# Latent attention with two sets of buffers and outputs through DRAM, and the triangular inverses' round trip on GpSimd's queue

## The chip, the cores and the metric

One core of one Trainium2 chip. The time is the device time of one execution in microseconds (us). An execution of the kernel before was timed three times; a further one was recorded by the profiler, and all rows below are from that one.

## What is computed

Two blocks of a small transformer on 256 tokens of width 2048, in float32. The first block (two layers of convolution and window attention) is not touched. The second block normalises, projects, runs two mixers on halves of the projection, joins their outputs in one out-projection and ends with a gated feed-forward part:

```python
proj = rms_norm(x, g) @ w_in
y_rwkv = rwkv7_mixer(...)     # 16 heads of 64: a recurrence over the tokens, group norm, gate
y_mla = mla_mixer(...)        # latent attention, 8 heads of 128, causal softmax
x = x + concatenate([y_rwkv, y_mla], -1) @ w_out      # 2048 -> 2048
...
# inside mla_mixer: q and k, v are projections of two latents c_q, c_kv of width 512
sc = (q_nope @ k_nope.T + q_pe @ k_pe.T) * scale
out = softmax(where(causal, sc, -1e30)) @ v           # for each head, in blocks of 128 queries
```

## The kernel before

Every large product is made in three passes: a weight tile comes from DRAM on SyncE's queue (`wraw`), ScalarE casts it to its high part `whi` (L285), VectorE subtracts to get the low part `wlo` (L286), and TensorE multiplies high by high, high by low and low by high. `lin` does so with 256 moving columns (L327 to L329), `wide` with the high and low half of the moving operand side by side (L347) and one pass for the low weights (L350). A moving operand is kept as such a pair of halves, a `Split`, in slots of 8 KB per partition; there are 8 slots (`slot`, tag x8), which the stages hand on to each other.

The function `mixers` makes the projection and both mixers. The recurrence goes over four groups G of four heads: `rwkv_lin` projects, `rwkv_prepare` makes the matrices of a group, among them, by `tri_inverse`, the inverses of small triangular matrices, and `rwkv_chunks` runs the four chunks of 64 tokens one after the other, each a chain of small matmuls (`pch`, L1106 to L1122) with copies on ScalarE between. `tri_inverse` writes the matrices to a DRAM buffer `xd` and reads them back in another layout as `L` (L1044, L1049, L1050), does 31 steps on VectorE (L1058, L1059; the starting `T` is loaded at L1053), writes the result to `td` (L1061), reads it back as `Tc` (L1063) and transposes it (L1064). These are 14 DMAs per group, 56 in all, issued by ScalarE: xd<-Lc is one of 1024 rows of 128 bytes, L<-xd are four of 32 rows and four of 512, td<-T four of 256 rows and Tc<-td one of 1024.

A group's output is gated by the product `pgt` (L1163, L1165), stored to the DRAM buffer `ydr` (L1166) and loaded back in `load_y` (L833), where `split_pair` makes the two halves: a cast on ScalarE (L271) and a subtraction on VectorE (L272). The four head pairs of the latent attention are made by `mla_pair`: projections, scores `msc` (L1306, L1307), the exponential and the scaling on ScalarE (L1313, L1318), transposes `mtr` (L1322), the products with the values `mo` (L1327 to L1329), and a copy of each head's output out of PSUM (L1330). All pairs work in the same two slots, `mla_s`, so one pair's buffers are let go before the next takes them. A pair's output `yp` is split straight from SBUF into its place in `Ym`.

The out-projection is `rows`: for each of eight column blocks j it multiplies first Ym (k = 0 to 7), then the first six tiles of Yr (the recurrence's output), and last, behind `load_y(3)`, tiles 6 and 7 by `lin`. It adds to the residual `h2`, two slots of 1 MB, loaded from `hdr` (L827) and scaled on VectorE (L829).

Instructions are put in order by a scheduler that runs when the program is built: it plays the program through on a model of the engines and writes one fixed order for each engine. The order in time on a queue is then that order; an instruction that waits holds back all that stand behind it on its engine. Parts of the recurrence have a higher priority in it (`high_priority`).

## Time and profile before

| | |
|---|---|
| median of three executions | 2218.68 us (2218.06 to 2219.01) |
| the profiled execution | 2222.46 us |
| its span, first to last instruction | 2220.7 us |
| mean granted clock of TensorE, share of full speed | 0.991 |
| TensorE busy | 2182.3 us, 98% |
| VectorE busy | 1698.3 us, 76% |
| ScalarE busy | 1186.7 us, 53% |
| GpSimd busy | 106.7 us, 5% |
| DMA traffic | 412.83 MB, 186 GB/s |

Engines are PE (TensorE), PEld (its weight loads), DVE (VectorE), ACT (ScalarE), POOL (GpSimd) and SP (SyncE); ACTq is ScalarE's queue as it issues DMAs. A line number is one of the kernel file. In timelines the square brackets give the idle time ahead of an instruction on its engine, and behind the arrow what ended it. Issuing a DMA isn't counted as busy on ScalarE.

### The profile page before, as it was taken

What the parts mean: (1) busy time and instruction counts of PE and PEld (TensorE: products, weight loads), DVE (VectorE), ACT (ScalarE), POOL (GpSimd) and SP (SyncE); (2) the same over time, 40 slices, a digit from 0 to 9 for tenths busy, and PEclk for the clock granted to TensorE, in tenths of its full rate; (3) what the DMA queues carried; (4) which work ended last, traced back from release to release, by engine and by line L of the source; (5) the groups of instructions that cost most, each with busy time, mean ns of one, the idle gap of its engine ahead of it and who ended that gap; (6) DMA issues with size and microseconds to landing.
All of it is one profiled execution on the core that took longest, in us unless ns stands there. A gap on an engine that the chain in (4) does not pass through costs nothing.

```text
span 2220.7 us, 37351 instructions
## 1 busy us (share of the span) xinstructions
PE 2182.3 (98%) x14263; PEld 1972.0 (89%) x14263; DVE 1698.3 (76%) x3140; ACT 1186.7 (53%) x1825; POOL 106.7 (5%) x253
## 2 busy tenths in 40 slices
PE   8999999999999999999999999999999999999998
PEld 8999988889999888899999887888888888888887
DVE  6999999778989988787777885777765576556765
ACT  6456746554456555656665655355443444444443
POOL 3100000000000000002100000010000000000000
PEclk9999999999999999999999998999999999999999
DMA  7875556665565466777665433576656666566654
GB/s 232 245 207 165 175 166 223 191 210 179 183 184 167 153 198 212 218 219 222 192 169 140 122 106 102 167 255 203 190 185 195 193 189 190 190 192 189 189 191 141
DMA packets 374514, 412.83 MB, mean 186 GB/s; under 512 B 40456, under 2 KB 327429, under 8 KB 373952
## 3 DMA queue, kind: packets, MB, share of 16 engines
q1 hardware_dynamic: 336464, 366.06, 53.6%
q0 software_dynamic: 10960, 31.79, 4.5%
q10 hardware_dynamic: 26912, 12.60, 2.6%
q8 instruction: 112, 1.84, 0.3%
q14 instruction: 66, 0.54, 0.1%
HBM read 390.47 MB, written 19.92 MB: 185 GB/s over the span
## 4 chain that ended last, share of the span: by engine, by line
PE 93%; DVE 3%; DMA 2%; ACT 1%; issue 1%; ACTq 0%; SPq 0%; DVEq 0%
PE wide L347 30%; PE wide L350 15%; PE lin L327 7%; PE lin L328 7%; PE lin L329 7%; PE lin L1393 3%; PE lin L1394 3%; PE lin L1392 3%; PE dn L1393 2%; PE dn L1394 2%; PE dn L1392 2%; PE po L701 1%; PE lin L1225 1%; PE lin L1223 1%; PE lin L1224 1%; DVE wlo L286 1%
## 5 line engine op out<-in xcount | busy, mean ns | idle before, releaser
L285 ACT CAST whi<-wraw 128x1024 fp32r<-128x1024 f32 (+1 forms) x708 | 724.8, 1026 | 837.7 <-PE wide L347 329.5
L286 DVE TENSOR_TENSOR wlo<-wraw,whi 128x1024 fp32r<-128x1024 f32 (+1 forms) x708 | 843.8, 1193 | 357.2 <-ACT whi L285 341.3
L347 PE MATMUL wide<-xs,whi 128*128 128x512 f32 x2916 | 745.7, 394 | 3.9 <-ACT whi L285 2.0
L347 PEld LDWEIGHTS wide<-xs,whi 128*128 128x128 f32 x2916 | 521.3, 189 | 95.0 <-ACT whi L285 2.5
L350 PEld LDWEIGHTS wide<-xs,wlo 128*128 128x128 f32 x2916 | 402.7, 190 | 33.0 <-DVE wlo L286 1.9
L350 PE MATMUL wide<-xs,wlo 128*128 128x256 f32 x2916 | 416.4, 283 | 0.4 <-DVE wlo L286 0.2
L329 PE MATMUL lin<-xs,wlo 128*128 128x256 f32 x1420 | 404.9, 285 | 2.2 <-DVE wlo L286 2.2
L327 PE MATMUL lin<-xs,whi 128*128 128x256 f32 x1420 | 405.5, 286 | 0.9 <-ACT whi L285 0.9
L328 PE MATMUL lin<-xs,whi 128*128 128x256 f32 x1420 | 404.7, 285 | 0.0
L329 PEld LDWEIGHTS lin<-xs,wlo 128*128 128x128 f32 x1420 | 273.5, 193 | 3.3 <-DVE wlo L286 2.6
L327 PEld LDWEIGHTS lin<-xs,whi 128*128 128x128 f32 x1420 | 273.4, 193 | 3.1 <-ACT whi L285 1.3
L328 PEld LDWEIGHTS lin<-xs,whi 128*128 128x128 f32 x1420 | 273.5, 193 | 1.1 <-issue 0.7
L583 DVE SCALAR_TENSOR_TENSOR cy<-apad,vc_cw,cy 128x256 f32<-128x256 f32 x480 | 229.7, 481 | 7.5
L1393 PE MATMUL lin<-wlo,xs 128*128 128x512 f32 (+1 forms) x304 | 117.7, 387 | 0.5 <-DVE wlo L286 0.5
L1394 PE MATMUL lin<-whi,xs 128*128 128x512 f32 (+1 forms) x304 | 117.0, 385 | 0.0
L1392 PE MATMUL lin<-whi,xs 128*128 128x512 f32 (+1 forms) x304 | 114.1, 386 | 0.2 <-ACT whi L285 0.2
L1393 PEld LDWEIGHTS lin<-wlo,xs 128*128 128x128 f32 x304 | 57.2, 188 | 11.9 <-DVE wlo L286 1.2
L1392 PEld LDWEIGHTS lin<-whi,xs 128*128 128x128 f32 x304 | 57.2, 188 | 11.6 <-ACT whi L285 0.6
L1392 PE MATMUL dn<-whi,xs 128*128 128x512 f32 (+1 forms) x176 | 67.0, 381 | 0.0
L1393 PE MATMUL dn<-wlo,xs 128*128 128x512 f32 (+1 forms) x176 | 67.0, 381 | 0.0
L1394 PE MATMUL dn<-whi,xs 128*128 128x512 f32 (+1 forms) x176 | 67.0, 381 | 0.0
L1394 PEld LDWEIGHTS lin<-whi,xs 128*128 128x128 f32 x304 | 57.2, 188 | 11.0
(540 smaller groups left out, 2374.4 us busy)
## 6 DMA issues: line engine op xcount, KB each, us to landing
wraw<-in_w_in_dram SPq DMA_DIRECT2D x244, 512.0 KB, 4.1
wraw<-in_w_out_dram SPq DMA_DIRECT2D x89, 512.0 KB, 4.2
wraw<-in_ffn_w_gate_dram SPq DMA_DIRECT2D x88, 512.0 KB, 4.4
wraw<-in_ffn_w_up_dram SPq DMA_DIRECT2D x88, 512.0 KB, 3.7
wraw<-in_ffn_w_down_dram SPq DMA_DIRECT2D x87, 512.0 KB, 3.9
wraw<-in_w_pg_dram SPq DMA_DIRECT2D x64, 512.0 KB, 4.3
bt<-btab POOLq DMA_DIRECT2D x32, 192.0 KB, 3.2
btab<-bF ACTq DMA_DIRECT2D x4, 1024.0 KB, 7.9
```

The lines of the kernel that those rows point to most:

```text
L285: nc.scalar.copy(hi[:], src)
L286: self.lo = nc.vector.tensor_tensor(lo[:], src, hi[:].bitcast(F32), ALU.subtract)
L327: nc.tensor.matmul(ps[:, t, :], lhsT=h, rhs=xh_, start=((t, k) == first), stop=False)
L328: nc.tensor.matmul(ps[:, t, :], lhsT=h, rhs=xl_, start=False, stop=False)
L329: nc.tensor.matmul(ps[:, t, :], lhsT=l, rhs=xh_, start=False, stop=((t, k) == last))
L347: nc.tensor.matmul(ps[t][:], lhsT=hi[:, i, ts], rhs=S.both(k).rearrange("p u c -> p (u c)"), start=(k == kts[0]), stop=False)
L350: nc.tensor.matmul(ps[t][:, :SEQ], lhsT=lo[:, i, ts], rhs=S.hi(k), start=False, stop=(k == kts[-1]))
L583: prev, tail = tail, nc.vector.scalar_tensor_tensor(y, ap[:, t, k : k + SEQ], cw[:, k : k + 1], y, ALU.mult, ALU.add)
L701: nc.tensor.matmul(po[:, qb, g, :], lhsT=pT[:, kb, qb * 128 : qb * 128 + 128], rhs=vd[:, kb, j, :], start=(kb == 0), stop=(kb == 1))
L1392: nc.tensor.matmul(ps, lhsT=zh, rhs=hi, start=(k == 0), stop=False)
L1393: nc.tensor.matmul(ps, lhsT=zh, rhs=lo, start=False, stop=False)
L1394: nc.tensor.matmul(ps, lhsT=zl, rhs=hi, start=False, stop=(k == nt - 1))
```

## The change

It does three things. The 14 DMAs of `tri_inverse` are issued by GpSimd in place of ScalarE. The latent attention gets two sets of its two slots, taken in turn by the pairs, and a pair's output is no longer split from SBUF: GpSimd stores it to a new DRAM buffer `mdr`, and `load_y` loads it back and splits it, for all four pairs ahead of the first three groups of Yr. The slots are taken in another order: Ym, h2, Yr behind the four slots of the attention, where it was mla, Ym, Yr, h2. An unused function is taken out, by which the lines behind it move up by 8 and, behind the new lines, by 5.

```diff
--- before.py
+++ after.py
...
@@ -812,28 +804,31 @@
         with self.tc.high_priority(offset=self.RP):
             self.rwkv_chunks(3, last)
         cq, ck = self.cqk
-        self.mla_s = self.slot(F32, "mla"), self.slot(F32, "mla")
-        Ym = self.new_split(2)
+        self.mla_s = [(self.slot(F32, "mla"), self.slot(F32, "mla")) for _ in range(2)]
+        self.mdr = self.dr.tile([128, 8, SEQ], F32, name="mdr")
         rf = self.wk.tile([128, SEQ], F32, tag="r", bufs=1, name="rf")
         self.bcast(self.rfc[:], None, out=rf)
         for hp in range(4):
-            self.mla_pair(hp, cq, ck, Ym)
+            self.mla_pair(hp, cq, ck)
 
         wo = A["w_out_2"][0]
+        Ym = self.new_split(2)
+        h2 = [self.slot(F32, "h2") for _ in range(2)]
         Yr = self.new_split(2)
-        h2 = [self.slot(F32, "h2") for _ in range(2)]
 
         for u in range(2):
             nc.gpsimd.dma_start(h2[u][:], self.hdr[:, 8 * u : 8 * u + 8, :])
             for k in range(8):
                 nc.vector.scalar_tensor_tensor(h2[u][:, k, :], h2[u][:, k, :], self.fg[:, 8 * u + k : 8 * u + k + 1], rf[:],
                                                ALU.mult, ALU.mult)
-        def load_y(G):
+        def load_y(G, dst, src):
             yt = self.sqt()
-            nc.gpsimd.dma_start(yt[:], self.ydr[:, 2 * G : 2 * G + 2, :])
-            self.split_pair(Yr, 2 * G, yt[:])
+            nc.gpsimd.dma_start(yt[:], src[:, 2 * G : 2 * G + 2, :])
+            self.split_pair(dst, 2 * G, yt[:])
+        for G in range(4):
+            load_y(G, Ym, self.mdr)
         for G in range(3):
-            load_y(G)
+            load_y(G, Yr, self.ydr)
         def rows(k0, k1, j, Y, row0=0):
             hh = self.at(h2, 2 * j, 2)
             if k1 - k0 < 4:
@@ -847,7 +842,7 @@
         late = 7
         for j in range(late):
             rows(0, 6, j, Yr)
-        load_y(3)
+        load_y(3, Yr, self.ydr)
         vf = self.vf
         self.x2 = self.dr.tile([128, KD, SEQ], F32, name="x2")
         self.XF = self.new_split()
@@ -1041,13 +1036,13 @@
         small = lambda s, tag="tri": self.wk.tile([128, 8, 32], F32, tag=tag, name=self.nm(s))
         Lc = small("Lc")
         nc.vector.tensor_tensor(Lc[:], AB[:, :, 0:32], AB[:, :, 32:64], ALU.add)
-        nc.scalar.dma_start(xd[:].rearrange("(c q) j i -> (q j) c i", q=4), Lc[:])
+        nc.gpsimd.dma_start(xd[:].rearrange("(c q) j i -> (q j) c i", q=4), Lc[:])
         L = self.wk.tile([128, 768], F32, tag="L", bufs=1, name=self.nm("L"))
         L0, L1 = L[:, 0:512].rearrange("p (j i) -> p j i", i=32), L[:, 512:768].rearrange("p (j i) -> p j i", i=16)
         for q in range(4):
             qs = slice(32 * q, 32 * q + 32)
-            nc.scalar.dma_start(L0[qs], xd[:, 0:16, :])
-            nc.scalar.dma_start(L1[qs], xd[:, 16:32, 16:32])
+            nc.gpsimd.dma_start(L0[qs], xd[:, 0:16, :])
+            nc.gpsimd.dma_start(L1[qs], xd[:, 16:32, 16:32])
         T, tmp = small("T"), small("Tt")
         o, n = CB["tinit"]
         nc.gpsimd.dma_start(T[:], self.A["c_blk"][:, o : o + n].rearrange("p (c i) -> p c i", c=8))
@@ -1058,9 +1053,9 @@
             nc.vector.tensor_tensor(tmp[:, 0:n, 0:m], lj, tj, ALU.mult)
             nc.vector.tensor_tensor(T[:, 0:n, j + 1 : 32], T[:, 0:n, j + 1 : 32], tmp[:, 0:n, 0:m], ALU.add)
         for q in range(4):
-            nc.scalar.dma_start(td[:, :, q, :], T[32 * q : 32 * q + 32, :, :])
+            nc.gpsimd.dma_start(td[:, :, q, :], T[32 * q : 32 * q + 32, :, :])
         Tc, Tt = small("Tc", "trc"), small("Ttr", "trc")
-        nc.scalar.dma_start(Tc[:], td[:].rearrange("(c h) e q i -> (h e q) c i", h=4))
+        nc.gpsimd.dma_start(Tc[:], td[:].rearrange("(c h) e q i -> (h e q) c i", h=4))
         nc.vector.transpose(Tt[:], Tc[:])
         return Tc, Tt
 
@@ -1246,12 +1241,12 @@
             hs = slice(64 * h, 64 * h + 64)
             nc.vector.tensor_tensor(kz[hs, h, :], tk[hs, 0, :], tk[hs, 1, :], ALU.add)
 
-    def mla_pair(self, hp, cq, ck, Y):
+    def mla_pair(self, hp, cq, ck):
 
         nc, A = self.nc, self.A
         wq, wkv = A["mla_w_uq_2"][0], A["mla_w_ukv_2"][0]
         cos, sin, kz, rc = self.cos, self.sin, self.kz, self.rkvc
-        s1, s2 = self.mla_s
+        s1, s2 = self.mla_s[hp % 2]
         qn, qp, kn, vn = (s1[:, 2 * u : 2 * u + 2, :] for u in range(4))
         yp, sh, pTs = s2[:, 0:2, :], [s2[:, 2:4, :], s2[:, 4:6, :]], s2[:, 6:8, :]
         scale = 192.0 ** -0.5
@@ -1328,7 +1323,7 @@
             nc.tensor.matmul(po[:, 128:256], lhsT=vn[:, 0, hs], rhs=pT[:, 0, 128:256], start=True, stop=False)
             nc.tensor.matmul(po[:, 128:256], lhsT=vn[:, 1, hs], rhs=pT[:, 1, 128:256], start=False, stop=True)
             nc.scalar.copy(yp[:, h, :], po[:])
-        self.split_pair(Y, 2 * hp, yp)
+        nc.gpsimd.dma_start(self.mdr[:, 2 * hp : 2 * hp + 2, :], yp)
 
 
     def ffn(self):
```

How the order of the instructions moves, at three places. First TensorE where the first pairs' outputs meet the out-projection. Before (`xs_14851` is the slot of Ym that holds k = 0 to 3, `mla_14850` and `mla_14849` the two slots of the pairs, `pch` the chunk chain of the last group):

```order
L347 MATMUL wide_15622<-xs_14851,whi_15628 128x512 x4
L350 MATMUL wide_15622<-xs_14851,wlo_15629 128x256 x3
L1322 MATMUL mtr_15393<-cblk,mla_14850 128x128 x2
L350 MATMUL wide_15622<-xs_14851,wlo_15629 128x256
L1106 MATMUL pch_14702<-rv,l_10987 128x64 x4
L1327 MATMUL mo_15374<-mla_14850,mla_14849 128x128
L1328 MATMUL mo_15374<-mla_14850,mla_14849 128x128
L1329 MATMUL mo_15374<-mla_14850,mla_14849 128x128
L347 MATMUL wide_15672<-xs_14851,whi_15678 128x512 x4
```

After (`xs_15585` is that slot of Ym; `mla_14849`, `mla_14850` are the first set and `mla_14851`, `mla_14852` the second; the first three rows end the attention of pair 1, and `msc_15378` are scores of pair 2; the two wide rows in the middle have k = 0 and 1, the last three k = 2 and 3):

```order
L1322 MATMUL mo_15217<-mla_14852,mla_14851 128x128
L1323 MATMUL mo_15217<-mla_14852,mla_14851 128x128
L1324 MATMUL mo_15217<-mla_14852,mla_14851 128x128
L1301 MATMUL msc_15378<-mla_14849 128x128
L1302 MATMUL msc_15378<-rope,mla_14849 128x128
L347 MATMUL wide_15637<-xs_15585,whi_15643 128x512 x2
L347 MATMUL wide_15687<-xs_15585,whi_15693 128x512 x2
L1301 MATMUL msc_15378<-mla_14849 128x256
L1302 MATMUL msc_15378<-rope,mla_14849 128x256
L347 MATMUL wide_15637<-xs_15585,whi_15643 128x512 x2
L350 MATMUL wide_15637<-xs_15585,wlo_15644 128x256 x4
L347 MATMUL wide_15687<-xs_15585,whi_15693 128x512 x2
```

The out-projection's matmuls on pair 1's output stand two scores and four matmuls behind that output's last matmul. Before, the first of them stood beside the last pair's attention and the chunk chain.

Second the queue of GpSimd at the same stretch. Before, the stores and loads of the recurrence with the residual's loads (h_2282, h_2283) behind the third store:

```order
L1166 DMA ydr<-sq_13236 128x512
L833 DMA sq_15614<-ydr 128x512
L1158 DMA ga_14839<-in_rwkv_g_2_dram 128x256
L1159 DMA ga_14839<-in_rwkv_g_2_dram 64x256
L1166 DMA ydr<-sq_14620 128x512
L827 DMA h_2282_15590<-hdr 128x2048
L827 DMA h_2283_15591<-hdr 128x2048
L833 DMA sq_15618<-ydr 128x512
L1166 DMA ydr<-sq_14810 128x512
L833 DMA sq_16316<-ydr 128x512
```

After:

```order
L1161 DMA ydr<-sq_13236 128x512
L820 DMA h_2282_15587<-hdr 128x2048
L1326 DMA mdr<-mla_14850 128x512
L820 DMA h_2283_15588<-hdr 128x2048
L826 DMA sq_15609<-mdr 128x512
L1326 DMA mdr<-mla_14852 128x512
L826 DMA sq_15613<-mdr 128x512
L1056 DMA td_14333<-T_14346 256x1x32 x4
L1153 DMA ga_14839<-in_rwkv_g_2_dram 128x256
L1154 DMA ga_14839<-in_rwkv_g_2_dram 64x256
L1161 DMA ydr<-sq_14620 128x512
L1326 DMA mdr<-mla_14850 128x512
```

The residual's two loads stand ahead of the load of the first pair's output and of the next pair's store; the third group's store of ydr now follows behind td.

Third TensorE where the last group's output meets the out-projection. Before, the product pgt of group 3 stood between wide matmuls on Ym:

```order
L347 MATMUL wide_15972<-xs_14852,whi_15998 128x512 x2
L1163 MATMUL pgt_14842<-hg,ga_14839 128x256 x4
L347 MATMUL wide_15972<-xs_14852,whi_15998 128x512 x2
L347 MATMUL wide_15973<-xs_14852,whi_15998 128x512 x4
```

After (`xs_15590` is the slot of Yr with k = 4 to 7):

```order
L350 MATMUL wide_16289<-xs_15590,wlo_16316 128x256 x2
L350 MATMUL wide_16290<-xs_15590,wlo_16316 128x256 x2
L1158 MATMUL pgt_14842<-hg,ga_14839 128x256 x4
L327 MATMUL lin_16340<-xs_15590,whi_16343 128x256
L327 MATMUL lin_16366<-xs_15590,whi_16369 128x256
L327 MATMUL lin_16394<-xs_15590,whi_16397 128x256
L328 MATMUL lin_16340<-xs_15590,whi_16343 128x256
```

The first LIN on the output of group 3 (tiles 6 and 7) follows directly behind that group's pgt; before, 60 rows stood between them.

## Rows read from the trace of the kernel before

**Rows 1.** The windows view: five engines in stretches of 100 us. Columns: the stretch; its length, then for TensorE (PE), its weight loads (PEld), VectorE (DVE), ScalarE (ACT) and GpSimd (POOL) the busy us and, in brackets, the instructions; then the granted clock of TensorE, the share of the DMA engines and GB/s.

```profile
1000.00:1100.00 100.00, 99.66 (x814) 97.70 (x813) 74.92 (x140) 63.04 (x95) 17.76 (x45) 1.00 0.74 213
1100.00:1200.00 100.00, 98.07 (x858) 94.27 (x857) 81.06 (x253) 61.59 (x105) 5.34 (x13) 0.98 0.58 154
1200.00:1300.00 100.00, 94.37 (x825) 84.03 (x824) 77.70 (x242) 59.93 (x126) 8.35 (x17) 0.95 0.42 112
1300.00:1400.00 100.00, 93.27 (x670) 81.45 (x669) 67.55 (x190) 52.04 (x122) 3.22 (x6) 0.90 0.40 124
```

**Rows 2.** The timeline of TensorE, those rows between 1100 and 1400 us with idle time ahead of them that the prediction names. Columns: start and duration in us, engine, line, operation, what it writes and reads, count; in square brackets the idle us ahead and what ended it.

```profile
1150.04 0.66 PE L1019 MATMUL ptn<-cblk,k__1748_12045 128*128 128x128 f32 x4 [1.41 <-DVE l L1034]
...
1210.11 0.39 PE L329 MATMUL lin<-xs,wlo 128*128 128x256 f32 x1 [1.64 <-DVE wlo L286]
...
1266.48 0.33 PE L1322 MATMUL mtr<-cblk,mla 128*128 128x128 f32 x1 [1.27 <-ACT mla L1318]
...
1280.39 0.93 PE L1114 MATMUL pch<-ch,tx 64*64 64x64 f32 x8 [1.31 <-ACT Y L1111]
...
1326.63 0.49 PE L1306 MATMUL msc<-mla 128*128 128x128 f32 x2 [0.92 <-DVE mla L1277]
1328.37 0.55 PE L1223 MATMUL lin<-ck,whi 128*128 128x256 f32 x1 [1.25 <-ACT mla L1297]
...
1337.19 1.11 PE L1163 MATMUL pgt<-hg,ga 128*128 128x256 f32 x3 [0.55 <-ACT sq L1155]
...
1363.59 0.84 PE L1322 MATMUL mtr<-cblk,mla 128*128 128x128 f32 x3 [1.86 <-ACT mla L1318]
1365.57 0.49 PE L1327 MATMUL mo<-mla,mla 128*128 128x128 f32 x2 [1.14 <-ACT mla L1324]
...
1367.62 1.97 PE L1106 MATMUL pch<-rv,l 128*128 128x64 f32 x8 [0.75 <-DVE rv L1129]
```

**Rows 3.** The timeline again, of VectorE (the first two rows) and of ScalarE. ACTq is the part of ScalarE's queue that issues DMAs.

```profile
1208.72 0.19 DVE L1058 TENSOR_TENSOR Tt<-L,T 128x31 f32<-128x31 f32 x1 [4.95 <-DMA L<-xd]
1208.83 1.22 DVE L286 TENSOR_TENSOR wlo<-wraw,whi 128x1024 fp32r<-128x1024 f32 x1
...
1259.86 2.56 ACTq L1061 DMA_DIRECT2D td<-T  x4
1262.74 0.40 ACT L1313 ACTIVATE mla<-mla,mst 128x128 f32<-128x128 f32 x1
...
1324.95 1.25 ACTq L1061 DMA_DIRECT2D td<-T  x2
1326.23 1.29 ACTq L1061 DMA_DIRECT2D td<-T  x2
1327.57 0.37 ACT L1330 COPY mla<-mo 128x256 f32<-128x256 f32 x1 [1.34 <-issue]
1327.83 0.48 ACT L1297 ACTIVATE mla<-lin,rkvc 128x256 f32<-128x256 f32 x1
```

**Rows 4.** The view of one buffer, of td and then of xd (the DRAM buffers of the inverse's round trip): line, queue, count, and the duration of one issue in ns (least, median, most).

```profile
L1061 ACTq DMA_DIRECT2D td<-T x16: 571/628/638, 1130.5 to 1326.9; - x16
L1063 ACTq DMA_DIRECT2D Tc<-td x4: 378/385/392, 1137.0 to 1332.1; - x4
...
L1049 ACTq DMA_DIRECT2D L<-xd x16: 308/497/1618, 1076.1 to 1285.7; - x16
L1050 ACTq DMA_DIRECT2D L<-xd x16: 322/445/832, 1076.8 to 1286.2; - x16
L1044 ACTq DMA_DIRECT2D xd<-Lc x4: 377/422/492, 1073.5 to 1279.2; - x4
```

**Rows 5.** The page's first part, GpSimd's row (busy us, share, instructions); the timeline of GpSimd, an issue of 128 rows; and the view of the buffer pr, whose load has 256 rows.

```profile
PE 2182.3 (98%) x14263; PEld 1972.0 (89%) x14263; DVE 1698.3 (76%) x3140; ACT 1186.7 (53%) x1825; POOL 106.7 (5%) x253
...
1070.37 0.54 POOL L1053 DMA_DIRECT2D T<-in_c_blk_dram  x1
...
L718 POOL DMA_DIRECT2D pr<-in_p_dram x2: 740/740/740, 17.5 to 254.9; - x2
```

**Rows 6.** The timeline around the last of the four round trips of a chunk group's output through DRAM, 256 KB, with a split behind it: TensorE, GpSimd (store and load), ScalarE, VectorE, and TensorE where the split is first read.

```profile
1414.68 2.00 PE L347 MATMUL wide<-xs,whi 128*128 128x512 f32 x8
...
1417.94 2.47 PE L1163 MATMUL pgt<-hg,ga 128*128 128x256 f32 x8
...
1421.69 0.55 POOL L1166 DMA_DIRECT2D ydr<-sq  x1 [62.83 <-DVE sq L1165]
1424.77 0.54 POOL L833 DMA_DIRECT2D sq<-ydr  x1 [2.53 <-DMA ydr<-sq]
...
1428.98 0.62 ACT L271 CAST xs<-sq 128x512 fp32r<-128x512 f32 x1 [1.22 <-DMA sq<-ydr]
...
1429.63 0.69 DVE L272 TENSOR_TENSOR xs<-sq,xs 128x512 fp32r<-128x512 f32 x1
...
1452.18 0.28 PE L327 MATMUL lin<-xs,whi 128*128 128x256 f32 x1
```

**Rows 7.** The view of the buffer hdr (the residual in DRAM): its loads, 1 MB each, and the landing times of its stores and loads; and the view of line 829, which scales what was loaded.

```profile
L827 POOL DMA_DIRECT2D h<-hdr x2: 534/536/537, 1342.5 to 1343.1; - x2
...
DMA to landing us min/median/max: 2.4/5.5/9.0
...
L829 DVE SCALAR_TENSOR_TENSOR h<-h,vc_a,rf x16: 475/478/480, 1359.4 to 1366.8; 128x256 f32<-128x256 f32 x16
```

**Rows 8.** The view of line 903, the longest copy that VectorE makes between buffers in this stage.

```profile
L903 DVE COPY rx<-rkt x4: 418/420/427, 1056.7 to 1261.5; 128x512 f32<-128x512 f32 x4
```

More of the change, by code (lines that the diff above doesn't have):

```diff
@@ L476, in bias_src @@
         return flat[127 : 127 + 128 * NREL].rearrange("(q c) -> q c", c=NREL)[:, :384]
-    def silu_pair(self, ps, r2, tag, bufs=2):
-        nc = self.nc
-        z = self.wk.tile([128, 2, SEQ], F32, tag=tag, bufs=bufs, name=self.nm("z"))
-        nc.vector.tensor_tensor(z[:], ps[:], r2, ALU.mult)
-        nc.scalar.activation(z[:], z[:], AF.Silu)
-        return z
     def gated(self, pv, pg, r2, other):
```

## The prediction

> **What bounds the kernel now.** I read the windows of 100 us first, then TensorE's idle times in the slow ones, and last the queues and the round trips that stand behind them. Outside the mixers of the second block TensorE has no gaps worth the name and its granted clock is at full speed, as in the window that begins at 1000 us (99.66% busy, clock 1.00) [rows 1]. In 1100 to 1400 it is idle for 1.93 + 5.63 + 6.73 = 14.3 us and the granted clock averages 0.98, 0.95 and 0.90 [rows 1]. At those clocks busy time of 98.07, 94.37 and 93.27 us does what full clock would do in 96.1, 89.7 and 83.9: some 16 us are lost to the clock. So at most 14.3 + 16 = 30 us can come back from this stage, and everything else is TensorE work that the change leaves as it is: the weight passes are the same.
>
> The idle times are short and each has its own releaser [rows 2]. Six of them, 7.0 us together, fall at 1150.04, 1210.11, 1266.48, 1326.63, 1328.37 and 1337.19; one of 1.31 us at 1280.39 stands inside the chunk chain; three, 1.86 + 1.14 + 0.75 = 3.75 us, stand at 1363 to 1368, in the attention of the last pair. Part of the six goes back to the triangular inverse's round trip on ACT's queue. At 1259.86 ACT's sequencer issues four DMAs for 2.56 us, and the exponential behind them starts at 1262.74; the transposes at 1266.48 wait for that chain. At 1324.95 and 1326.23 it issues 1.25 + 1.29 us, and the scaling at L1297 that releases TensorE at 1328.37 starts at 1327.83 [rows 3]. DVE, being in order, waits 4.95 us at 1208.72 for L<-xd [rows 3], and the wlo at 1210.11 that TensorE waits for stands right behind it.
>
> **The change, part by part.**
>
> *56 issues leave ACT.* 16 x 0.628 + 4 x 0.385 + 16 x 0.497 + 16 x 0.445 + 4 x 0.422 = 28.3 us of ACT's queue [rows 4]. ACT's own work has slack on the whole, so what this returns is the part of the six idle times that such an issue or its wait ended: between 0 and 7.0 us. I take 6, near the upper end, because at three of them the rows show the issue or the wait directly ahead. The wait for L<-xd doesn't vanish, but in the new order DVE has other work in that place. The clock returns some of its 16 us: the windows show the lower clock in the stretches that have these idle times. Of 1200:1300 and 1300:1400 (4.7 + 9.3 us) those of the chunk chain and of the last pair's attention keep theirs; I take 6 of 0 to 16.
>
> *The same 56 on GpSimd.* GpSimd is busy 5% of the span [rows 5], so the time is there; what counts is its order. A 128-row issue takes 0.54 us there, one of 256 rows 0.74 [rows 5]. L<-xd, td<-T and Tc<-td move tiny rows, up to 1024 of 128 bytes, and no row shows such an issue on this queue: at the lower end they stay at 0.74 us, by the slope between the two (0.20 us for 128 rows) a 1024-row one takes 1.9, in proportion to the rows 3.0. I take the slope, since two of the fourteen DMAs in a group reach that size; the round trip of the inverse is then some 2 to 3 us longer per group. For three of four groups it has tens of us of other work around it and costs nothing; if that cover is gone it costs its full length. For the last it is part of the next term.
>
> *Attention, its outputs by way of DRAM (the first two places of the order).* Before, a pair's output is split from SBUF into hi and lo straight behind the copy out of PSUM. Now it is copied (0.37 us [rows 3]), stored by GpSimd, loaded, cast on ACT and subtracted on DVE. The chunk groups' outputs make a round trip of this form and size; of the last one the store ydr<-sq is issued at 1421.69, the load at 1424.77, the cast starts at 1428.98 and the subtraction ends at 1430.32 [rows 6]: 8.6 us, 9.0 with the copy. The new order puts WIDE with k = 2, 3 (the second pair) only four WIDE and four score matmuls behind that pair's last output: 4 x 0.25 [rows 6] + 2 x 0.49 [rows 2] = 2.0 us of work to hide 9.0. That alone is 7.0 us of idle TensorE. The queue ahead of it makes it worse. On GpSimd the load of the residual's second half (1 MB) stands ahead of the loads of both pairs, and it waits for the last chunk group but one to let go of its buffer; the two loads of this kind landed after up to 9.0 us [rows 7]. On DVE its eight scalings, 8 x 0.478 us [rows 7], stand ahead of the low half of the first pair and of pair 2's score maxima. 9.0 + 3.8 = 12.8 us against some 6 us of TensorE work is 7 us more, but it runs at the same time as the round trip: I take 9 for the two (7.0 to 14). The last pair's round trip has 6 us of matmuls behind it, so 3 more. And the attention of pairs 2 and 3 now runs with next to no chunk steps between: the last pair alone cost 3.75 us that way before [rows 2], I take 8 for two (4 to 8). That is 20 us, less the 3.75 that are there already: **+16** (+3 to +21).
>
> *The last chunk group's output (third place).* The pgt matmuls of group 3 used to end 34 us ahead of the first LIN on Yr's k = 6, 7 (1417.94 to 1452.18 [rows 6]). The order now puts that LIN directly behind pgt. Its path is DVE's product, store, load, cast, subtraction: issue 1421.69 minus pgt's end 1420.41, plus 8.6 [rows 6], some 9.9 us, of which the first cast's products can start a little earlier: **+9** (7 to 11).
>
> *The clock after the new idle times.* Behind the idle times of now the granted clock falls to 0.90 over the window 1300:1400 [rows 1], 9.3 us for 6.7 us of idle time. The new ones are longer but in two places only. I take +3 (0 to 9).
>
> *The rest at nothing*: the two more buffers are slots of the same pool that lie free or are let go by then, and the order of the weight stream is unchanged; if a buffer came free later, the wait would be at the residual's loads, which is counted.
>
> Sum: -6 - 6 + 16 + 9 + 3 = **+16**. The profiled execution took 2222.46 us (span 2220.7), 3.8 above the median of the runs, 2218.68; the difference goes on the median: **2235**. About 0.2% (4.4 us) can be told from no change, so the bounds are 2214.2 and 2223.1.
>
> By the Trainium skill ("SBUF — State Buffer", section "SBUF: two separate sides") a DMA issued from GpSimd has its descriptors written by GpSimd's cores, which are locked out while DVE runs a copy or cast in its two-port mode, and one issued from ACT or SP is not. The trace so far does not bear it out: issues on this queue take 0.53 to 0.54 us [rows 5, 7] with DVE 68 to 75% busy [rows 1]. The longest DVE copy between buffers takes 0.42 us [rows 8]; by the rule 56 issues that each met one would take an estimated 24 us more, of which only what lies ahead of TensorE counts.
>
> **The rivals.**
>
> A, faster. The gains come in full (7 + 16 = 23 us) and the attention's term is nearly free, because with buffers of their own the pairs' scores and exponentials run ahead of TensorE and the order's closeness is not closeness in time. For it: the four WIDE with k = 0, 1 also wait, and so pair 1's trip can lie under that wait. Against: that wait is idle time itself. With +4 for that term and +9 at LIN the time is 2218.7 - 23 + 13 = 2209. It decides as long as that term is below 9.6 us (23 - 9 - 4.4).
>
> B, slower still. The moved issues are slow, by the number of rows or because DVE keeps them waiting. In proportion to rows (0.74 us for 256) a group's fourteen take 17.0 us (3.0 + 3.0 + 4 x 0.74 + 4 x 1.48 + 4 x 0.54), 9.9 more than the 7.1 on ACT; with GpSimd in order the stores of Y, the residual's loads and the pairs' trips are late by it. If 5 us of that show in three groups, 2235 + 15 = 2250. Against: the issues of now are flat.
>
> C, about the same. The attention's term at +8, since the residual's load is early enough, gains of 8 + 10, LIN +9: 2218.7 - 18 + 17 + 2 = 2220.
>
> That the change would not do what it says is excluded by the order: 56 issues fewer on ACT's queue, 64 more on GpSimd's.
>
> **How the numbers follow.** The forecast has 0.60, A 0.12, B 0.16, C 0.12. Faster by over 0.2% is A: 0.12. Same is most of C and a tail of the forecast: 0.13. Slower: 0.75. The forecast's own bounds are -23 to +44 with every term at an end, which no one case gives; with terms halfway to their ends it is 2222 to 2250. The range takes in C and most of B and leaves out A and B's tail: 2216 to 2256.
>
> **What would show it.** Right: two idle times of 7 us or more, at WIDE on the second pair's output and at the first LIN behind pgt, both released by the low or high half of xs; 1100 to 1300 at 99% busy and clock near 1.00; ACT's queue without L1044 to L1063; GpSimd waiting for DMAs. Wrong: the LIN of k = 6, 7 starting within 3 us of pgt; the idle times of 1150 to 1337 unchanged (then ACT's queue was not their cause); GpSimd's issues of L<-xd above 1.9 us (B); more idle time at the chunk chain than before.

## The result and the profile after

The changed kernel takes 2236.32 us (median of four runs, 2233.81 to 2239.04); before takes 2218.37 beside it. The ratio is 1.0081, with 95% confidence 1.0067 to 1.0094: 15 to 21 us slower. The profiled execution took 2233.96 us with a span of 2232.2, so the two traces differ by 11.5 us, less than the medians do: the trace of before is of an execution 4.1 above the median beside the change, that of after 2.4 below.

The windows of after, columns as in [rows 1]:

```profile
1100.00:1200.00 100.00, 100.00 (x892) 96.82 (x891) 83.91 (x252) 66.46 (x112) 18.08 (x34) 1.00 0.57 159
1200.00:1300.00 100.00, 95.00 (x839) 84.22 (x838) 78.96 (x231) 57.71 (x120) 20.83 (x37) 0.98 0.41 121
1300.00:1400.00 100.00, 87.16 (x589) 74.08 (x590) 64.26 (x195) 48.46 (x115) 11.91 (x21) 0.88 0.44 140
1400.00:1500.00 100.00, 88.45 (x531) 76.44 (x530) 72.06 (x138) 45.36 (x70) 11.21 (x23) 0.95 0.53 169
```

and the one of before that wasn't shown:

```profile
1400.00:1500.00 100.00, 97.04 (x571) 83.74 (x569) 77.08 (x141) 49.05 (x73) 12.33 (x25) 1.00 0.66 215
```

Against [rows 1] the time from 1100 to 1200 has no idle time left (1.93 before), 1200 to 1300 has 5.00 (5.63), 1300 to 1400 has 12.84 (6.73) and 1400 to 1500 has 11.55 (2.96). That is 12.1 us more idle time. Busy time times what the clock lacks is 0 + 1.9 + 10.5 + 4.4 = 16.8 us, against 2.0 + 4.7 + 9.3 + 0 = 16.0: in these two executions the clock as a whole gave nothing back.

By stage, idle time and clock together, the two traces differ by -7.3 us from 1100 to 1300, +7.2 from 1300 to 1400 and +13.0 from 1400 to 1500.

TensorE's waits in those windows, as in [rows 2] (with pgt of the last group, which doesn't wait, ahead of the last):

```profile
1240.51 0.38 PE L1218 MATMUL lin<-cq,whi 128*128 128x256 f32 x1 [2.18 <-ACT whi L285]
...
1278.94 0.39 PE L1220 MATMUL lin<-ck,wlo 128*128 128x256 f32 x1 [1.09 <-DVE wlo L286]
...
1332.37 2.07 PE L347 MATMUL wide<-xs,whi 128*128 128x512 f32 x4 [5.71 <-DVE xs L272]
...
1337.97 1.22 PE L347 MATMUL wide<-xs,whi 128*128 128x512 f32 x2 [1.82 <-DVE xs L272]
...
1354.31 1.17 PE L1317 MATMUL mtr<-cblk,mla 128*128 128x128 f32 x4 [2.05 <-ACT mla L1313]
...
1372.41 2.08 PE L347 MATMUL wide<-xs,whi 128*128 128x512 f32 x4 [2.01 <-DVE xs L272]
...
1451.14 2.47 PE L1158 MATMUL pgt<-hg,ga 128*128 128x256 f32 x8
1461.85 1.01 PE L327 MATMUL lin<-xs,whi 128*128 128x256 f32 x3 [8.23 <-ACT xs L271]
```

The six idle times of [rows 2] at 1150 to 1337 are gone, 7.0 us; others stand in 1200 to 1300, 5.0 us together, the longest at 1240 and 1279. The new ones are at WIDE on the first and second pair's output (5.71 + 1.82), at the transposes of the last pair (2.05), at WIDE on the last pair's output (2.01) and, directly behind pgt, at LIN (8.23). What runs on VectorE ahead of the first of them, with ScalarE's cast of the first pair's output to its high half as the last row:

```profile
1320.71 0.48 DVE L822 SCALAR_TENSOR_TENSOR h<-h,vc_a,rf 128x256 f32<-128x256 f32 x1 [1.05 <-DMA h<-hdr]
...
1321.18 2.84 DVE L822 SCALAR_TENSOR_TENSOR h<-h,vc_a,rf 128x256 f32<-128x256 f32 x7
...
1327.27 3.25 DVE L822 SCALAR_TENSOR_TENSOR h<-h,vc_a,rf 128x256 f32<-128x256 f32 x8
1330.55 0.42 DVE L1303 CUSTOM_DVE_ANT_0 mla<-msc,cblk 128x256 f32<-128x256 f32 x1
...
1331.64 0.68 DVE L272 TENSOR_TENSOR xs<-sq,xs 128x512 fp32r<-128x512 f32 x1
...
1327.26 0.62 ACT L271 CAST xs<-sq 128x512 fp32r<-128x512 f32 x1 [2.20 <-DMA sq<-mdr]
```

The residual's scalings (h<-h) take 0.48 + 2.84 + 3.25 us here, and the last eight stand in one piece ahead of the second score maximum and of the low half that WIDE waits for (1331.64). The cast that this low half needs had ended at 1327.88, 3.8 us sooner. GpSimd over the same time:

```profile
1312.54 0.55 POOL L820 DMA_DIRECT2D h<-hdr  x1 [16.60 <-PE lin L1220]
1313.08 0.54 POOL L1326 DMA_DIRECT2D mdr<-mla  x1
1319.60 0.53 POOL L820 DMA_DIRECT2D h<-hdr  x1 [5.98 <-PE pch L1101]
1321.77 0.54 POOL L826 DMA_DIRECT2D sq<-mdr  x1 [1.63 <-DMA mdr<-mla]
```

The second load of the residual waits 5.98 us for the chunk group, and the load of the first pair's output is issued behind it. So two explanations offer themselves for the 5.71 us, VectorE's order and GpSimd's; the experiments have to part them. The moved issues, in the view of xd and of td, answer to [rows 4]:

```profile
L1044 POOL DMA_DIRECT2D L<-xd x16: 502/509/537, 1076.8 to 1288.1; - x16
L1045 POOL DMA_DIRECT2D L<-xd x16: 652/657/684, 1077.3 to 1288.6; - x16
L1039 POOL DMA_DIRECT2D xd<-Lc x4: 903/918/972, 1073.8 to 1281.4; - x4
...
L1056 POOL DMA_DIRECT2D td<-T x16: 569/596/628, 1128.0 to 1344.7; - x16
L1058 POOL DMA_DIRECT2D Tc<-td x4: 910/913/915, 1133.0 to 1349.6; - x4
```

### The profile page after: what moved, and what is told of

Read it like the earlier page. It is cut to its first block, busy times and chain, and to the rows that moved or that the text cites. A ratio compares the mean times of both kernels' runs of the same rounds, so it can differ in the third digit from the quotient of the medians.

```text
span 2232.2 us, 37347 instructions
## 1 busy us (share of the span) xinstructions
PE 2181.7 (98%) x14263; PEld 1970.5 (88%) x14263; DVE 1702.1 (76%) x3140; ACT 1187.6 (53%) x1825; POOL 145.9 (7%) x317
```

## The experiments

All times are medians; before took 2217.8 to 2219.3 us beside them. Ratios are to before, with their 95% interval. The idle sums are of 1100 to 1400 unless told.

**The inverses' DMAs alone**, all five lines of `tri_inverse` that issue them, in the kernel before:

```diff
-        nc.scalar.dma_start(xd[:].rearrange("(c q) j i -> (q j) c i", q=4), Lc[:])
+        nc.gpsimd.dma_start(xd[:].rearrange("(c q) j i -> (q j) c i", q=4), Lc[:])
...
```

> Only the inverses' 56 DMAs move from ScalarE's to GpSimd's queue; the latent attention is as before. Theory 1 (the idle times at 1150 to 1337 belong to ScalarE's queue, and the slower time of the whole change to the DRAM trips): they go, as they did in the whole change, and nothing takes their place, since 45 rows stand between pgt of group 3 and the first LIN: 2211 us (2205 to 2216), idle time in 1100 to 1400 down from 14.3 to 5 to 9 us. Theory 2 (they went because the attention pairs have buffers of their own): no change, 2218. Theory 3 (GpSimd's slower issues hold up the chunk chain): 2222 or more, with idle time at pz or pch.

2219.59 us, ratio 1.0005 (0.9996 to 1.0013): no change. Idle time fell from 14.3 to 9.9 us, near what theory 1 had, but the windows show what came for it:

```profile
1100.00:1200.00 100.00, 100.00 (x891) 96.69 (x889) 83.90 (x253) 66.43 (x112) 18.44 (x35) 1.00 0.57 160
1200.00:1300.00 100.00, 93.05 (x714) 81.13 (x713) 69.41 (x209) 51.09 (x106) 21.01 (x37) 0.83 0.35 104
1300.00:1400.00 100.00, 97.05 (x759) 85.13 (x759) 76.68 (x220) 56.99 (x134) 7.03 (x12) 1.00 0.43 137
```

The granted clock of 1200 to 1300 is 0.83 in this execution, and TensorE waits in that stretch at other places:

```profile
1268.87 0.68 PE L1114 MATMUL pch<-ch,tx 64*64 64x64 f32 x8 [1.27 <-ACT Y L1111]
...
1277.46 1.07 PE L1082 MATMUL pz<-Ttr,XOc 32*32 32x32 f32 x32 [1.57 <-DVE Ttr L1064]
...
1279.29 1.19 PE L1000 MATMUL pbn<-sq,cblk 128*128 128x256 f32 x2 [0.77 <-DVE tx L1034]
```

The transpose Ttr of group 2 now starts at 1276.88 us (1268.17 before), and pz waits for it. The other two idle times shown stand in the recurrence too. It isn't GpSimd's issues that make the inverse late: the last load of L for this group is issued at 1204.46 (1204.51 before), but VectorE starts the first of the 31 steps at 1217.22, where before it started it at 1208.72 [rows 3], as soon as L had landed. The order that the scheduler wrote for VectorE has it later.

So freeing ScalarE's queue moved a part of the idle time, and the time is the same. The lower clock is not one execution's alone: the eleven of this run have a mean granted clock of 0.9908, the 31 of before beside them 0.9925. By an estimate, 0.0017 of 2219 us, that is 3.8 us, and TensorE's idle time over the whole span is 2.3 us less (36.1 against 38.4). Theory 1 falls, since the gain that I had counted in full doesn't come; theory 2 has the time, but not for its reason, since the idle times went without the attention's buffers; theory 3 has the wait at pz without the loss.

**The attention's part alone**: the whole change, with those five lines as before:

```diff
-        nc.gpsimd.dma_start(xd[:].rearrange("(c q) j i -> (q j) c i", q=4), Lc[:])
+        nc.scalar.dma_start(xd[:].rearrange("(c q) j i -> (q j) c i", q=4), Lc[:])
...
```

> Only the attention's part: two sets of buffers, outputs through DRAM, the slots' new order; the inverses' DMAs stay on ScalarE's queue. Theory 1: the idle times of before at 1150 to 1337 stay, the waits at the first pairs' outputs come (5 to 8 us net), and the 8.2 us at LIN do not, since it takes td and Tc of group 3 behind the attention's DMAs on GpSimd's queue to bring them (57 rows stand between pgt of group 3 and LIN here): 2226 us (2221 to 2231). Theory 2 (the DRAM trips bring all of it): 2236 or more, with 8 us idle at LIN.

2220.76 us, ratio 1.0009 (1.0000 to 1.0017). LIN doesn't wait, as theory 1 said, but the whole is 5 us better than it said. WIDE doesn't wait either. The second eight scalings (1327.54) stand ahead of a step of the attention on VectorE (L1274) here, and TensorE waits 4.73 us for it at the scores (1331.18) and 2.70 at the transposes behind them. The idle time of 1300 to 1400 is 12.22 us, nearly that of the change (12.84), so that stretch's idle time by itself doesn't tell the loss. The two parts cost 0.4 and 1.6 us alone and 18 together: the loss is an interaction.

**The whole change, the residual's loads and scalings later in the program.**

```diff
-        for u in range(2):
-            nc.gpsimd.dma_start(h2[u][:], self.hdr[:, 8 * u : 8 * u + 8, :])
-            for k in range(8):
...
         for G in range(4):
             load_y(G, Ym, self.mdr)
+        for u in range(2):
+            nc.gpsimd.dma_start(h2[u][:], self.hdr[:, 8 * u : 8 * u + 8, :])
+            for k in range(8):
...
```

> The whole change, but the residual's two loads and their scalings stand behind the loads of the attention's outputs in the program. Theory 1 (the wait at WIDE with k = 0, 1 is that for the residual's load and its scalings, ahead of the outputs on GpSimd's and VectorE's queues): the 5.7 us fall under 1, the wait at k = 2, 3 stays at most 4, and pgt stands 17 rows ahead of LIN, so that 8.2 us there fall to about 4: 2227 us (2222 to 2232). Theory 2 (it is the round trip's own length): the 5.7 us move to k = 2, 3, and the time is 2232 or more.

2219.95 us, ratio 1.0001 (0.9992 to 1.0009). All 17 us are back, more than theory 1 had. WIDE on the first pair doesn't wait, and LIN, with 7.9 us of matmuls between it and pgt, waits 0.77 us:

```profile
1437.74 2.48 PE L1158 MATMUL pgt<-hg,ga 128*128 128x256 f32 x8
...
1448.87 0.50 PE L327 MATMUL lin<-xs,whi 128*128 128x256 f32 x2 [0.77 <-ACT xs L271]
```

The outputs' way through DRAM is still there, so its length is not what costs.

**One set of buffers, the rest as in the change.**

```diff
-        self.mla_s = [(self.slot(F32, "mla"), self.slot(F32, "mla")) for _ in range(2)]
+        self.mla_s = [(self.slot(F32, "mla"), self.slot(F32, "mla"))] * 2
```

> The whole change, but all pairs work in one set of two slots, as before; outputs still go through DRAM. The residual's loads then find free slots and are done long before. Theory 1 (what costs is that the second set takes the slots of the residual and of Ym, and the order that follows; the DRAM trip as such is hidden): 2214 us (2208 to 2221), idle at WIDE on the pairs' outputs under 4 us in all and none at LIN (57 rows between). Theory 2 (the DRAM trip costs its length at the pairs' outputs whatever the slots): 2228 or more.

2228.91 us (2218.06 to 2232.43; two of the eight executions at 2218 and 2220, the others at 2227 to 2232), ratio 1.0037 (1.0020 to 1.0054): between the theories. The places that both named don't wait much (WIDE 1.86 us, LIN none), but the scalings moved up to 1259.88 to 1268.3 us, ahead of the end of group 2's inverse, and a chunk step waits 5.49 us for VectorE at 1268.78. With one set a loss stays, at another place: a third order has its own wait. That two sets needn't cost anything was shown by the run before this one.

**The scalings later in the program, the loads where they were.**

```diff
         for u in range(2):
             nc.gpsimd.dma_start(h2[u][:], self.hdr[:, 8 * u : 8 * u + 8, :])
-            for k in range(8):
...
             load_y(G, Ym, self.mdr)
+        for u in range(2):
+            for k in range(8):
...
```

> The whole change with the residual's loads where they are, on GpSimd's queue ahead of the outputs' loads, and only their sixteen scalings on VectorE (6.1 us) moved behind the loads of the outputs. GpSimd's order is that of the whole change, and LIN still stands directly behind pgt of group 3. Theory 1 (VectorE's order: the scalings ahead of the low half of the first pair): the 5.7 us at WIDE with k = 0, 1 fall to 2 to 3, the 8.2 us at LIN stay, since it is the round trip alone that stands there: 2232 us (2228 to 2235). Theory 2 (GpSimd's order: the loads ahead hold up the outputs' loads): 5 us or more stay at WIDE, 2235 or more. Theory 3 (both stalls are VectorE's): 2224 or less.

2235.18 us, ratio 1.0082 (1.0068 to 1.0096). It looks like theory 2 and is no test: the scheduler put the scalings where they had been (the first starts at 1320.87, 1320.71 in the change), as VectorE's timeline shows.

```profile
1327.47 3.26 DVE L829 SCALAR_TENSOR_TENSOR h<-h,vc_a,rf 128x256 f32<-128x256 f32 x8
...
1331.85 0.68 DVE L272 TENSOR_TENSOR xs<-sq,xs 128x512 fp32r<-128x512 f32 x1
```

It counts as a second measurement of the change.

**td and Tc back on ScalarE's queue.**

```diff
-            nc.gpsimd.dma_start(td[:, :, q, :], T[32 * q : 32 * q + 32, :, :])
+            nc.scalar.dma_start(td[:, :, q, :], T[32 * q : 32 * q + 32, :, :])
...
-        nc.gpsimd.dma_start(Tc[:], td[:].rearrange("(c h) e q i -> (h e q) c i", h=4))
+        nc.scalar.dma_start(Tc[:], td[:].rearrange("(c h) e q i -> (h e q) c i", h=4))
```

> The whole change, but td<-T and Tc<-td (20 of the 56 DMAs) go back to ScalarE's queue; xd and L stay on GpSimd's. Theory 1 (the 8.2 us at LIN come from group 3's td and Tc standing behind the attention's DMAs on GpSimd's queue): Tc of group 3 is issued some 8 us sooner than at 1349.6, 45 rows stand between pgt and LIN, no idle time there: 2226 us (2221 to 2230). Theory 2 (they come from VectorE's and TensorE's order, whatever the queue): 2233 or more.

2220.58 us, ratio 1.0010 (1.0001 to 1.0019). LIN starts 21.7 us behind pgt's end (1428.17) and doesn't wait:

```profile
1449.85 0.28 PE L327 MATMUL lin<-xs,whi 128*128 128x256 f32 x1
```

Better than theory 1 by 5 us, though WIDE on the second pair's output waits 3.68 us here. Its step on the time was only half right: Tc of group 3 is issued at 1345.71, 3.9 us sooner, and its T is as late as in the change (1341.51 against 1342.51).

**td and Tc alone on GpSimd's queue**, in the kernel before:

> The kernel before with td<-T and Tc<-td alone on GpSimd's queue; xd and L stay on ScalarE's, the attention as before. By the run that moved all 56 (no change, since group 2's and 3's inverses came 7 to 9 us later), moving only the part that holds ScalarE in blocks of 2.5 us should keep the gain (1.3 + 1.3 us of idle at 1266 and 1328) and delay the inverses by less: 2216 us (2212 to 2219). If GpSimd's path delays them as much, no change or slower: 2219 to 2223.

2216.55 us, ratio 0.9990 (0.9981 to 0.9999): the gain is 2 to 3 us, at the edge of what can be told.

**The attention's part alone with the residual later**, the second and the third edit together:

> The attention's part of the change alone with the residual's loads and scalings behind the loads of its outputs; the inverses' DMAs on ScalarE's queue. Theory 1 (the place of the residual's work and the inverses' queue make up the whole loss, the DRAM trips are covered): 2217 us (2213 to 2221), idle in 1300 to 1400 below 8 us. Theory 2 (the trips cost by themselves some 5 us): 2223 or more.

2219.92 us, ratio 1.0008 (0.9999 to 1.0017): no change. Idle in 1300 to 1400 is 11.67 us, not below 8; the time sides with theory 1, the idle time with neither.

**The scalings tied on VectorE behind the second pair's low half**, GpSimd's order left with the loads ahead:

```diff
+        lows = [load_y(G, Ym, self.mdr) for G in range(4)]
         for u in range(2):
             for k in range(8):
-                nc.vector.scalar_tensor_tensor(h2[u][:, k, :], h2[u][:, k, :], self.fg[:, 8 * u + k : 8 * u + k + 1], rf[:],
+                s = nc.vector.scalar_tensor_tensor(h2[u][:, k, :], h2[u][:, k, :], self.fg[:, 8 * u + k : 8 * u + k + 1], rf[:],
...
+                self.behind(s, lows[1])
```

`behind` gives the scheduler a dependency that only sets the order of two instructions.

> The run that moved only the scalings in the program left them where they were in VectorE's order (the first still at 1320.87 us). Here each of the sixteen is tied behind the low half of the second pair's output on VectorE; GpSimd's queue keeps the residual's loads ahead of the outputs' loads. Theory 1 (VectorE's order: 6.1 us of scalings stand ahead of the low half of the first pair, the score maxima and the steps of group 3's inverse): WIDE with k = 0, 1 waits under 2 us, T of group 3 is ready near 1335 in place of 1342.5, 45 rows stand between pgt and LIN and nothing waits there: 2221 us (2217 to 2226). Theory 2 (the loads ahead on GpSimd's queue): 5 us or more still stand at WIDE, 2228 or more.

2217.99 us, ratio 0.9994 (0.9985 to 1.0004): the whole loss is gone, as theory 1 had it. GpSimd's part of the timeline is that of the change, the wait of 6 us and the late load included:

```profile
1314.76 0.55 POOL L820 DMA_DIRECT2D h<-hdr  x1 [16.60 <-PE lin L1221]
1315.30 0.55 POOL L1327 DMA_DIRECT2D mdr<-mla  x1
1321.82 0.53 POOL L820 DMA_DIRECT2D h<-hdr  x1 [5.97 <-PE pch L1102]
1324.24 0.54 POOL L823 DMA_DIRECT2D sq<-mdr  x1 [1.89 <-DMA mdr<-mla]
```

VectorE now has the low halves at 1330.37 and 1338.39 first, and then the scalings (a long row of them shown):

```profile
1330.37 0.69 DVE L272 TENSOR_TENSOR xs<-sq,xs 128x512 fp32r<-128x512 f32 x1
...
1338.39 0.69 DVE L272 TENSOR_TENSOR xs<-sq,xs 128x512 fp32r<-128x512 f32 x1 [1.50 <-ACT xs L271]
...
1340.40 4.04 DVE L828 SCALAR_TENSOR_TENSOR h<-h,vc_a,rf 128x256 f32<-128x256 f32 x10
```

On TensorE neither WIDE on the first pair (the order has it four score matmuls later) nor LIN waits:

```profile
1331.12 1.26 PE L347 MATMUL wide<-xs,whi 128*128 128x512 f32 x4
...
1424.49 2.47 PE L1159 MATMUL pgt<-hg,ga 128*128 128x256 f32 x8
...
1448.64 0.28 PE L327 MATMUL lin<-xs,whi 128*128 128x256 f32 x1
```

So theory 2 is out: the loads on GpSimd's queue are the same and cost no time. What the tie changes is VectorE's order and, since the scheduler runs again, TensorE's with it: pgt ends 21.7 us ahead of LIN. The run doesn't part these two. TensorE still waits, 8.92 us in 1300 to 1400 (6.73 before), the longest 2.52 at the attention's products with the values (1335.90).

**Tied behind the first pair's low half only.**

```diff
-                self.behind(s, lows[1])
+                self.behind(s, lows[0])
```

> As the run that ties the residual's scalings behind the low half of the second pair, but behind that of the first pair alone: they then stand ahead of the second pair's low half and of the last steps of group 3's inverse, and LIN again stands directly behind pgt of group 3. Theory 1 (the loss has two places, each by its neighbours in the order): the 5.7 us at WIDE with k = 0, 1 fall under 2, the 8.2 us at LIN stay: 2228 us (2224 to 2232). Theory 2 (one delay that shows in two places: when the first wait goes, the second goes too): 2222 or less, with under 2 us at LIN.

2224.48 us, ratio 1.0026 (1.0017 to 1.0035), inside theory 1's numbers: WIDE on the first pair doesn't wait, LIN stays directly behind pgt and waits the same 8.23 us.

```profile
1328.27 0.69 DVE L272 TENSOR_TENSOR xs<-sq,xs 128x512 fp32r<-128x512 f32 x1 [0.32 <-ACT xs L271]
...
1328.00 0.70 PE L1302 MATMUL msc<-mla 128*128 128x256 f32 x2 [1.57 <-DVE mst L1304]
...
1329.01 1.20 PE L347 MATMUL wide<-xs,whi 128*128 128x512 f32 x4
1333.66 1.09 PE L1318 MATMUL mtr<-cblk,mla 128*128 128x128 f32 x3 [3.45 <-ACT mla L1314]
...
1336.78 0.80 PE L1323 MATMUL mo<-mla,mla 128*128 128x128 f32 x2 [2.03 <-ACT mla L1320]
...
1441.66 2.48 PE L1159 MATMUL pgt<-hg,ga 128*128 128x256 f32 x8
1452.37 1.01 PE L327 MATMUL lin<-xs,whi 128*128 128x256 f32 x3 [8.23 <-ACT xs L271]
```

```profile
1300.00:1400.00 100.00, 90.21 (x650) 77.49 (x648) 70.69 (x203) 52.71 (x121) 11.94 (x21) 0.95 0.48 152
```

GpSimd's load of the first pair's output is issued at 1321.82 (1321.77 in the change) and its cast starts at 1327.61 (1327.26), so the two traces can be laid side by side: without the scalings ahead the low half starts 3.4 us sooner (1328.27 against 1331.64). The rest of the 5.71 us lies in TensorE's order, which now has four score matmuls ahead of WIDE. But the idle time up to 1339 is not less: 1.57 + 3.45 + 2.03 and 0.46 at 1338.89 are 7.5 us, against 5.71 + 1.82. The scalings now stand ahead of the softmax's reciprocals on VectorE (1333.02), and the attention waits in WIDE's place.

With this run the loss has two parts. Each against before of its own round, the change is 18.0 us slower, this run 6.7, and the run before it 0.7 faster: LIN directly behind pgt is worth some 7 us, and the scalings ahead of the first low half some 11. (The last two runs differ in 1300 to 1400 too, where LIN isn't.) What the parts consist of shows when idle time and clock are put beside the times. Idle time is the span less TensorE's busy time in the trace; the clock is the mean over all executions that list it.

| | us against before | idle time, us | mean granted clock |
|---|---|---|---|
| before | 0 | 38.4 | 0.9925 (0.9924 to 0.9929 by round) |
| the whole change | +18.0 | 50.5 | 0.9888 |
| inverses' DMAs alone | +0.4 | 36.1 | 0.9908 |
| attention's part alone | +1.6 | 41.0 | 0.9925 |
| the whole change, residual later | +0.8 | 37.2 | 0.9931 |
| scalings behind the first low half | +6.7 | 46.8 | 0.9928 |
| scalings behind the second low half | -0.7 | 38.0 | 0.9930 |

By an estimate 0.001 of clock is 2.2 us, and with it idle time and clock add up to each time within 3.5 us. LIN's part is idle time (46.8 - 38.0 = 8.8 us at an equal clock). The part of the scalings is 3.7 us of idle time and, by the estimate, 9 us of clock. In the traces of these two the idle time of 1300 to 1400 falls by 3.1 us (12.84 to 9.79) and the clock there rises from 0.88 to 0.95, which is 10.5 - 4.5 = 6 us. Why idle times of nearly the same length, at other places, leave the clock so different is not shown.

**Two tries for a faster kernel.** td and Tc on GpSimd with the residual later, in the kernel before:

> The kernel before with td<-T and Tc<-td on GpSimd's queue and, in the program, the residual's loads and scalings behind the first three loads of Yr. In the order the loads stand one place later on GpSimd. If the residual's place also cost something in the kernel before (the last pair's attention with 3.75 us idle): 2213 us (2210 to 2217), below the 2216.6 of td and Tc alone. If it is only the second set that puts it in the way: the same 2216.6 within 2.

2215.45 us, ratio 0.9982 (0.9973 to 0.9990): the fastest here, 0.18% below before. Against the 2216.55 of td and Tc alone that is 1.1 us, so what was to be parted is not.

The tied scalings with only td and Tc on GpSimd:

> The attention's part of the change with the scalings tied behind the second pair's low half, and of the inverses' DMAs only td and Tc on GpSimd's queue. If the double buffers are worth anything once the residual's work is out of the way, it is below the 2215.5 of the best run so far: 2213 us. But only 4 rows stand between pgt of group 3 and LIN here, and by the dependence seen so far (8.2 us with none between, 0.8 with 17) some 6 us of idle time come back there: 2221 us (2217 to 2225), the likelier.

2225.83 us, ratio 1.0039 (1.0027 to 1.0052), 0.8 us above the upper end of the likelier case. LIN stands four rows further back than in the change and waits 6.72 us, as the distances had it:

```profile
1453.79 1.01 PE L327 MATMUL lin<-xs,whi 128*128 128x256 f32 x3 [6.72 <-ACT xs L271]
```

Over all runs, by the time that TensorE works between the end of pgt and LIN: with none LIN waits 8.23, 8.27 and 8.23 us; with 1.4 us 6.72; with 7.9 us 0.77; with 11.5 (both runs with td and Tc in the kernel before) and with 21.7 and more, none. Work and wait together are 8.1 to 8.7 us each time that it waits: the length of the round trip. Here T of group 3 was ready at 1332.13, ten us sooner than in the change, and LIN waited all the same; with td and Tc back on ScalarE it was late and LIN didn't wait. So what makes the scheduler set the last chunk group late is not T's readiness on the chip. It stays open.

## Why the prediction was right, and where it was not

The time (2235 against 2236.3) and the two places are right. That the sum came out is partly luck. Its idle terms, -6 + 16 + 9, make 19 us, and the traces have 12.1 more; its clock terms, -6 + 3, give 3 back, and the clock took some 8 (0.9888 against 0.9925, an estimate). The two errors cancel.

- *LIN directly behind pgt, +9*: measured 8.23 us of idle time, worth some 7 us of time between two runs. Right, mechanism and size: the order of TensorE told it. (The reading of before is off: 1417.94 is where pgt starts, and from its end to LIN are 31.8 us, not 34.)
- *The waits at the pairs' outputs*: named at WIDE, found at WIDE, but not on the same pair. I had 7 us or more on the second pair's output; it is 5.71 on the first pair's and 1.82 on the second's. As a sum I took 9 for the first two pairs (7.53 measured) and 3 for the last (2.01). I put the scalings beside the length of the round trip and the queue of GpSimd as three causes that overlap. The run with the tied scalings shows that one decides: with the same round trips and the same GpSimd order there is no loss. The second pair's trip is long here, 1328.15 (its copy) to 1337.91 (its low half), 9.8 us against my 9.0, and of nearly the same length in that run (1330.25 to 1339.08), where no WIDE waits for it.
- *Attention of pairs 2 and 3, 8 us*: too much; TensorE's waits inside it are 2.05 us and some below 0.5. The term of +16 in all measures +8.8 in idle time: 12.84, less the 6.73 - 2.72 of before that are not among the six idle times of the first term.
- *56 issues off ScalarE, -6, and -6 of clock*: the terms that failed. The six idle times went, 7.0 us, 4.3 of them in 1100 to 1300; but that stretch as a whole has only 2.6 us less (5.0 against 7.6), since TensorE waits at other places there, and where I named 99% busy as the sign, 1200 to 1300 has 95. The clock there gave back 4.8 us in the traced pair, and 1300 to 1500 took 5.6. The run with these issues alone is worth 0 (0.9996 to 1.0013), at a mean clock below that of before, and the clock over all executions of the change fell where I had it rise. An idle time that goes is no gain if its work was on a chain that waits at its next link.
- *The clock after the new idle times, +3*: too small. From 1400 to 1500, behind LIN's wait, it is 4.4 us, none before.
- *GpSimd's issues*: the lower end was nearest. 0.51 us for 32 rows of 2 KB, 0.66 for 512 of 64 bytes, 0.60 for 256 of 128 bytes (td) and 0.92 for 1024, against 1.9 by my slope. A group's fourteen take 0.92 + 4 x 0.51 + 4 x 0.66 + 4 x 0.60 + 0.91 = 8.9 us, 1.8 more than on ScalarE. Rival B is out.
- The Trainium skill's rule on GpSimd's descriptors ("SBUF — State Buffer", section "SBUF: two separate sides") was not put to the test, and the prediction's "does not bear it out" says too much. VectorE's plain copies of before and after, 0.28 to 0.42 us, are few, and in the trace of after those between 1050 and 1350 (at 1056.7, 1115.9, 1148.7, 1177.8, 1194.6, 1229.4 and 1261.9) meet none of the moved issues, which lie within 59 ns of each other for td and 35 and 32 for L.
- The forecast's outer bounds were added wrongly: its own terms at their ends give -13 to +41, not -23 to +44, and halfway 2220 to 2247, not 2222 to 2250. The range was set by the rivals that it takes in.

Of the 6.5 us by which the profiled pair differs less than the medians (11.5 against 18.0), the clock explains most, by the same estimate: the trace of before is of an execution at 0.991, that of after of one at 0.990, where the means are 0.9925 and 0.9888. The clock's part rests on values of three digits, and only one execution of each kernel has a trace. Open is also what makes the scheduler set the last chunk group where it does.

## What to carry over

Read the order of each engine for what stands directly ahead of a long wait: a consumer that stands right behind its producer's round trip waits its whole length; 11.5 us of other work between hid it here, 7.9 nearly. When several queues are late at one place, tie one instruction group behind the late result and leave the rest: that parted VectorE's scalings (the whole loss, by way of the orders that follow from them) from GpSimd's loads (none). And before a freed queue is counted as a gain, follow the chain to its next link.

## What was not expected of the hardware

A GpSimd issue grows little with its rows: 0.51 us for 32 rows of 2 KB, 0.92 for 1024 of 128 bytes; on ScalarE the medians were 0.50 and 0.42 [rows 4]. And the granted clock moves the time as much as the idle time does, without following it: with 3.1 us less idle time in 1300 to 1400, 6 us came back through the clock, while the attention's part alone has 12.22 us idle there and a mean clock of 0.9925, that of before.
